# Six products without weight sums at the head of the first block, and weight parts of two pairs made one product later

## The chip, the cores and the metric

The kernel runs on one core of one Trainium2 chip. The metric is the device time of one execution in microseconds; several executions are made, and their median is given. Times inside an execution come from the hardware profiler and count from the start of the span.

## The reference

The program is a bidirectional encoder trunk of two layers on 512 tokens plus 16 learned meta tokens, with 1024 channels. Each layer is a feed-forward block, a mixer of two parallel branches (gated linear attention and grouped-query attention), and a second feed-forward block. The change touches the feed-forward block alone:

```python
def swiglu(x, w_gate, w_up, w_down):
    return (jax.nn.silu(x @ w_gate) * (x @ w_up)) @ w_down

h = h + 0.5 * swiglu(rmsnorm(h, norm_gains[l, 0]), ffn_w_gate[l, 0], ffn_w_up[l, 0], ffn_w_down[l, 0])
h = h + mixer(rmsnorm(h, norm_gains[l, 1]), ...)
h = h + 0.5 * swiglu(rmsnorm(h, norm_gains[l, 2]), ffn_w_gate[l, 1], ffn_w_up[l, 1], ffn_w_down[l, 1])
```

The hidden width is 2816, which is 22 tiles of 128 columns. The kernel works them as 11 pairs; a pair is two hidden tiles, gate and up.

## The kernel before

Each float32 matmul is made of three matmuls in a faster format: an operand is split into a high part (`whi` for a weight, made by ScalarE, L227) and a low part (`wlo`, made by VectorE from the weight and the high part, L228), and high by high, high by low and low by high are summed in PSUM.

For gate and up of a pair, the weight is cut into four blocks 11, 12, 21, 22, and the tokens into two halves. Instead of eight block products, seven are formed, by a Winograd scheme. They are called 1 to 7. Products 1, 2 and 4 use the blocks 11, 12 and 22 as they come from HBM (`DIRECT`). Products 5, 6, 7 and 3 use sums and differences of blocks. Those sums are built in SBUF: ScalarE writes the negative of block 11 or 12 (L178), SP loads a base block (L173), and the GpSimd queue issues DMAs that add a block or another sum onto it (L183). For one pair the chain is: negative of 11, add 21 to it (this is the weight of 7), add that to a loaded 22 (the weight of 6), add 22 to a loaded 21 (the weight of 5), and add the weight of 6 to the negative of 12 (the weight of 3). Each of these transfers is 512 KB.

One product is 24 matmuls of TensorE (L516) into two PSUM banks. Of a pair, products 1, 6, 7 and 4 add up in the same banks X; ScalarE copies X out after 1, 6 and 7 (`snapshot`, L522). Product 2 has banks Y. Products 5 and 3 add up in banks Z; before 3 may start, VectorE has read Z together with the copy that was made after 7 (L534). `hidden` then applies the norm factor `rs`, the gate function and the product, and splits the result for the down projection (L393). PSUM holds two double banks for even pairs (`s2`) and two for odd ones (`ss`).

The norm factor `rs` of the block is made from the squares of the input (ScalarE L427, added up by VectorE L431), a matmul with a constant (L399), and a few steps on ScalarE and VectorE (L405, L376, L409 to L411). The opening block computes the squares at product 5 of pair 0.

`ffn_steps` lists the products and the down projection's steps of a block; the same list makes the plan of weight loads, in the order of use. When product j is emitted, `Weights.use` emits the making of the parts of all products before j + `AHEAD_MADE` (4) and the loads of all before j + `AHEAD_FETCHED` (6). `whi` and `wlo` have four buffers each, raw weights three, the negatives three, the loaded bases two. A scheduler then orders each engine's queue; the engines work their queues in order.

In this text 1·6 is product 6 of pair 1, and so on. The first of a block's groups has the pairs 0 to 3.

Of the kernel before, what the change touches and what calls it, by code (L numbers as in the profile page):

```python
# [14 lines left out]
ALU = mybir.AluOpType  # L15
AX = mybir.AxisListType

P = 128
D = 1024
KC = D // P  # L20
# [13 lines left out]
AHEAD_MADE = 4  # L34
# [11 lines left out]
DIRECT = {"1": "11", "2": "12", "4": "22"}  # L46


def ffn_steps():


    steps, pair = [], 0
    for g, n in enumerate(GROUPS):

        ahead = g == 0
        steps += [("P", p, c) for p in range(pair, pair + 1 + ahead) for c in "12"]
        steps += [("P", pair, c) for c in "65"]
        for i in range(n):
            p, more = pair + i, i + 1 < n
            early = [[("P", p + 1, "1")], [("P", p + 1, "2")]] if more else \  # L60
                [[("D", g, 0, 0, 2 * n - 2)], [("D", g, 1, 0, 2 * n - 2)]]
            if ahead and i == 0:
                early = [[], []]
            steps += early[0] + [("P", p, "7")] + early[1] + [("P", p, "4"), ("P", p, "3")]
            if more:
                steps += [("P", p + 1, "6"), ("P", p + 1, "5")]
        steps += [("D", g, m, 0, 2 * n - 2) for m in range(2, HELD)]
        steps += [("D", g, m, 2 * n - 2, 2 * n) for m in range(HELD)]
        steps += [("D", g, m, 0, 2 * n) for m in range(HELD, KC)]
        pair += n  # L70
    return steps


def weight_plan():


    plan = []

    def mat(name, idx, col, k0, nk, width=P):
        for k in range(k0, k0 + nk):  # L80
            plan.append(("tile", name, idx, k * P, col, width))

    def ffn(l, f):
        for step in ffn_steps():
            if step[0] == "P":
                plan.append(("op", (l, f)) + step[1:])
            else:
                _, g, m, first, last = step
                mat("ffn_w_down", (l, f), m * P, 2 * sum(GROUPS[:g]) + first, last - first)

    gate_cols = [c + m * P for m in range(KC) for c in (O_GA, O_GB)]
    for l in range(DEPTH):
        ffn(l, 0)
        cols = [O_R + i * P for i in range(4)]
        for c in cols:
            mat("w_in", (l,), c, 0, KC)
# [12 lines left out]
    return plan  # L109
# [38 lines left out]
class Weights:  # L148
# [83 lines left out]
            if not isinstance(load, int) and load[2] in "12":  # L232
                self.sums(*load, w)

    def use(self, j):
        self.make(j + AHEAD_MADE)
        self.fetch(j + AHEAD_FETCHED)
        return self.got[j]

# [15 lines left out]
        self.pos += n - 1  # L255
        return [t[:, c : c + n * width] for t in self.got[self.at[s]]]

    def op(self, *load):

        assert PLAN[self.pos][1:] == load, (PLAN[self.pos], load)  # L260
        self.pos += 1
        return [t.rearrange("p (w k m) -> p w k m", w=2, k=KC // 2) for t in self.use(self.at[load])]


def build(tc, ctx, xt, wts, win, par, w2, const, umask, out):
    nc = tc.nc
    V, S, G, TE = nc.vector, nc.scalar, nc.gpsimd, nc.tensor
# [10 lines left out]
    W = Weights(nc, pool("wraw", 3), pool("whi", 4), pool("wlo", 4), wts, win)  # L278
# [217 lines left out]
    def ffn(l, f, norm, done, following):  # L496

        x, rs, n = norm.x, None, live[0]
        w = n // 2
# [3 lines left out]
        def product_of_pair(p, product):  # L503
            kind = "s2" if p % 2 == 0 else "ss"
            st = made.setdefault(p, {})
            where, begin = {"1": ("X", 1), "6": ("X", 0), "7": ("X", 0), "4": ("X", 0), "2": ("Y", 1), "5": ("Z", 1),
                            "3": ("Z", 0)}[product]
            if begin:
                st[where] = pair(kind == "s2")
            acc = st[where][:, :, :w]  # L510
            hi, lo = W.op((l, f), p, product)
            at = PLACE[product]
            for k, (xh, xl) in enumerate(x):
                for j in range(2):
                    for i, (a, b) in enumerate(((hi, xh), (hi, xl), (lo, xh))):
                        TE.matmul(acc[:, j], a[:, j, k], b[:, at], start=bool(begin and k == 0 and i == 0),  # L516
                                  stop=k == len(x) - 1 and i == 2, skip_group_check=not begin)

            def snapshot(name):
                t = slots["snap"].tile([P, T], F32, tag="snap", name=nm("snap"))[:, :n]  # L520
                st[name] = v2(t)
                S.copy(st[name], acc)  # L522

            if product == "1":
                snapshot("p1")
            elif product == "2":
                c = slots["c"].tile([P, 4 * T], F32, tag="c", name=nm("c"))[:, : 4 * n]
                st["c"] = c.rearrange("p (j q c) -> p j q c", j=2, q=4)
                V.tensor_tensor(st["c"][:, :, 0], st["p1"], acc, ALU.add)
            elif product == "6":  # L530
                snapshot("q")
            elif product == "7":
                snapshot("r")
                V.tensor_tensor(st["c"][:, :, 3], st["r"], st["Z"][:, :, :w], ALU.add)  # L534
            elif product == "4":
                hidden(st, p, 1)
            elif product == "3":
                V.tensor_tensor(st["c"][:, :, 1], st["q"], acc, ALU.add)
                hidden(st, p, 0)

        def hidden(st, p, m):

            c = st["c"]
            t, u = [c[:, j, 2 * m : 2 * m + 2].rearrange("p q c -> p (q c)") for j in range(2)]
            x21 = st["X"][:, :, :w]
            cuts = [(t, u, t, u, slice(0, n))] if m == 0 else \
# [28 lines left out]
            if g == len(GROUPS) - 1:  # L575
                (done or finish_chunk)(m)

        steps = ffn_steps()
        last_op = max(i for i, t in enumerate(steps) if t[0] == "P")
        for i, step in enumerate(steps):  # L580
            if step[0] == "P":
# [596 lines left out]
```

## Time and profile before

| what | us |
|---|---|
| median of three runs | 2242.1 (2241.26 to 2243.97) |
| the profiled execution's own time | 2245.28 |
| its span on the profiler | 2243.5 |
| TensorE busy / idle in the span | 2199.7 / 43.8 |
| VectorE, ScalarE, GpSimd busy | 1522.7, 1196.9, 154.1 |
| mean granted TensorE clock | 0.995 |

A row of the page or of a timeline names the engine, the line, the operation, what it writes and reads (`ss<-xc,whi` is a product of input parts and a weight's high part into PSUM), the shape and the count; in square brackets stands how long the engine was idle before it and what ended that. PEld is the weight load of TensorE, SPq and ACTq are DMA issues. A row of stretches gives the stretch, its length, and for PE, PEld, DVE, ACT and POOL the busy time and the number of instructions, then the granted clock, the busy share of the DMA engines and GB/s. `w<-win` is a weight block from HBM, `s<-w` and `w<-s` are transfers between sums. Line numbers are those of the kernel before; the changed kernel has the same lines some 3 to 13 further on.

### The profile page before, as it was taken

To read this page: it belongs to the slowest core of one execution; us is meant where nothing else is said; L and a number is where in the kernel's file an instruction comes from. 1 tells how busy PE (TensorE), PEld (TensorE's weight loads), DVE (VectorE), ACT (ScalarE), POOL (GpSimd) and SP (SyncE) were. 2 spreads that over 40 slices of the span, in tenths; PEclk is the share of its full clock that TensorE was granted. 3 is DMA by queue.
4 is the path that set the end of the run, shared out by engine and by line. 5 is a ranking of instruction groups with operands and counts; after the bars stand their busy time and mean duration, and the time that the engine had idled before them with its cause. 6 is when DMAs were issued, how large, how long until landed. Compare 5 with 4: busy or idle time off the path is not lost.

```text
span 2243.5 us, 39771 instructions
## 1 busy us (share of the span) xinstructions
PE 2199.7 (98%) x16506; PEld 2094.6 (93%) x16506; DVE 1522.7 (68%) x2415; ACT 1196.9 (53%) x1769; POOL 154.1 (7%) x180
## 2 busy tenths in 40 slices
PE   6999999999999999999999999999999999999998
PEld 5999999989999999999999999999788888989897
DVE  6656567586886676565696575675878767756566
ACT  7635355454785564454575363553457836636353
POOL 1101010000000010101011110100000001101010
PEclk9999999999999999999999999999999999999999
DMA  9859563212113475766667685632121136859662
GB/s 252 217 151 221 150 175 99 85 48 70 48 40 110 132 201 157 189 178 179 171 173 198 162 220 140 173 105 76 52 80 48 48 123 170 215 149 226 152 177 66
DMA packets 88613, 315.58 MB, mean 141 GB/s; under 512 B 9840, under 2 KB 12272, under 8 KB 88432
## 3 DMA queue, kind: packets, MB, share of 16 engines
q1 hardware_dynamic: 61136, 218.26, 29.2%
q0 software_dynamic: 25344, 92.29, 23.0%
q8 instruction: 129, 2.11, 0.4%
q10 hardware_dynamic: 1952, 2.50, 0.3%
q14 instruction: 52, 0.43, 0.1%
HBM read 264.77 MB, written 2.10 MB: 119 GB/s over the span
## 4 chain that ended last, share of the span: by engine, by line
PE 86%; DVE 6%; ACT 4%; DMA 2%; issue 1%; SPq 0%; DVEq 0%; ACTq 0%; POOLq 0%
PE ss L516 37%; PE ss L393 26%; PE mm L393 13%; PE sm L393 2%; DMA w<-win 2%; DVE wlo L228 1%; PE sm L893 1%; PE ss L868 1%; ACT whi L227 1%; ACT t L376 1%; PE sm L909 1%; PE sm L910 1%; PE ss L869 1%; PE ss L399 1%; PE sm L718 0%
## 5 line engine op out<-in xcount | busy, mean ns | idle before, releaser
L516 PE MATMUL ss<-xc,whi 128*128 128x264 f32 (+1 forms) x4928 | 905.4, 285 | 22.7 <-ACT whi L227 14.9
L516 PEld LDWEIGHTS ss<-xc,whi 128*128 128x128 f32 x4928 | 768.1, 189 | 27.2 <-ACT whi L227 15.3
L516 PE MATMUL ss<-xc,wlo 128*128 128x264 f32 (+1 forms) x2464 | 702.3, 285 | 3.8 <-DVE wlo L228 3.8
L393 PE MATMUL ss<-g,whi 128*128 128x264 f32 (+2 forms) x2692 | 495.3, 300 | 0.0
L516 PEld LDWEIGHTS ss<-xc,wlo 128*128 128x128 f32 x2464 | 466.5, 189 | 5.9 <-DVE wlo L228 5.6
L393 PEld LDWEIGHTS ss<-g,whi 128*128 128x128 f32 x2692 | 391.4, 188 | 16.2
L393 PE MATMUL mm<-x,whi 128*128 128x264 f32 (+1 forms) x1712 | 384.5, 315 | 0.0
L227 ACT CAST whi<-w 128x1024 fp32r<-128x1024 f32 (+1 forms) x221 | 231.0, 1046 | 265.4 <-PE ss L393 117.7
L227 ACT CAST whi<-raw 128x1024 fp32r<-128x1024 f32 x190 | 199.4, 1049 | 292.8 <-PE mm L393 97.5
L228 DVE TENSOR_TENSOR wlo<-w,whi 128x1024 fp32r<-128x1024 f32 (+1 forms) x221 | 267.9, 1219 | 110.3 <-ACT whi L227 108.5
L393 PE MATMUL ss<-g,wlo 128*128 128x264 f32 (+2 forms) x1346 | 312.2, 300 | 0.0
L228 DVE TENSOR_TENSOR wlo<-raw,whi 128x1024 fp32r<-128x1024 f32 x190 | 232.2, 1222 | 95.5 <-ACT whi L227 94.0
L393 PEld LDWEIGHTS mm<-x,whi 128*128 128x128 f32 x1712 | 278.3, 188 | 16.6 <-issue 1.0
L393 PE MATMUL mm<-x,wlo 128*128 128x264 f32 (+1 forms) x856 | 265.9, 315 | 0.0
L393 PEld LDWEIGHTS ss<-g,wlo 128*128 128x128 f32 x1346 | 215.7, 188 | 8.3
L227 ACT CAST whi<-s 128x1024 fp32r<-128x1024 f32 x88 | 92.5, 1051 | 151.1 <-PE ss L516 131.4
L228 DVE TENSOR_TENSOR wlo<-s,whi 128x1024 fp32r<-128x1024 f32 x88 | 107.6, 1223 | 96.2 <-ACT whi L227 96.1
L393 PEld LDWEIGHTS mm<-x,wlo 128*128 128x128 f32 x856 | 159.5, 188 | 8.4 <-issue 0.7
L483 DVE SCALAR_TENSOR_TENSOR t<-ss,rs 128x528 f32<-128x528 f32 (+1 forms) x93 | 64.6, 701 | 127.1 <-PE ss L393 127.0
L178 ACT ACTIVATE s<-w 128x1024 f32<-128x1024 f32 x88 | 93.3, 1060 | 74.7 <-DMA w<-win 40.4
L183 POOL DMA_DIRECT2D w<-win x44 | 39.1, 889 | 944.7 <-DVE wlo L228 439.5
L522 ACT COPY snap<-ss 128x528 f32<-128x528 f32 (+1 forms) x132 | 77.1, 584 | 1.2 <-PE ss L516 1.2
(245 smaller groups left out, 2568.7 us busy)
## 6 DMA issues: line engine op xcount, KB each, us to landing
w<-win SPq DMA_DIRECT2D x219, 512.0 KB, 4.7
raw<-wts SPq DMA_DIRECT2D x190, 512.0 KB, 3.4
s<-win POOLq DMA_DIRECT2D x44, 512.0 KB, 6.8
w<-s POOLq DMA_DIRECT2D x44, 512.0 KB, 5.5
w<-win POOLq DMA_DIRECT2D x44, 512.0 KB, 7.2
s<-w POOLq DMA_DIRECT2D x44, 512.0 KB, 7.4
h<-xt SPq DMA_DIRECT2D x3, 528.0 KB, 6.9
out<-h ACTq DMA_DIRECT2D x4, 256.0 KB, 2.3
```

Source lines behind the costliest of these rows:

```text
L178: self.nc.scalar.activation(t, w, AF.Copy, scale=-1.0)
L183: self.nc.gpsimd.dma_start(t, src, accum_op=ALU.add)
L227: nc.scalar.copy(hi[:, cs], w[:, cs])
L228: nc.vector.tensor_tensor(lo[:, cs], w[:, cs], hi[:, cs].bitcast(F32), ALU.subtract)
L376: prev_act[0] = S.activation(*args, **kw).ins
L393: TE.matmul(acc.half[i][:width], lhs, rhs[:, acc.spans[i]], start=first, stop=last)
L399: TE.matmul(a, weights, x[:, hs], start=True, stop=True)
L483: V.scalar_tensor_tensor(cut(dst[rows]), pv[rows], -0.5 * f, cut(rs[rows]), ALU.mult, ALU.mult)
L516: TE.matmul(acc[:, j], a[:, j, k], b[:, at], start=bool(begin and k == 0 and i == 0), stop=k == len(x) - 1 and i == 2, skip_group_check=no ...
L522: S.copy(st[name], acc)
L868: TE.matmul(s[:n, i, :HF], lhs, kh[:, hs], start=True, stop=False)
L869: TE.matmul(s[:n, i, :HF], lhs, kl[:, hs], start=False, stop=True)
```

## The change

`ffn_steps` gets a flag that is set for the first block of the program alone. There, product 4 of pairs 0 and 1 stands right behind products 1 and 2 of both pairs, so that the block begins with 0·1, 0·2, 1·1, 1·2, 0·4, 1·4. Such a product 4 can't be added onto X, which holds product 1 alone at that time. It is summed in banks of its own (W), ScalarE copies it out, and after product 7 VectorE adds the copy of X to it; `hidden` of that half follows product 7 and reads the sum from SBUF. Besides, in pairs 0 and 1 of every block the parts are made one product later (`AHEAD_MADE` - 1). The core of the diff:

```diff
-def ffn_steps():
+def ffn_steps(opening):
...
         steps += [("P", p, c) for p in range(pair, pair + 1 + ahead) for c in "12"]
+        early4 = (0, 1) if opening and ahead else ()
+        steps += [("P", p, "4") for p in early4]
         steps += [("P", pair, c) for c in "65"]
...
-            steps += early[0] + [("P", p, "7")] + early[1] + [("P", p, "4"), ("P", p, "3")]
+            steps += early[0] + [("P", p, "7")] + early[1] + [("P", p, c) for c in "43" if c == "3" or p not in early4]
...
-    def use(self, j):
-        self.make(j + AHEAD_MADE)
+    def use(self, j, ahead=AHEAD_MADE):
+        self.make(j + ahead)
         self.fetch(j + AHEAD_FETCHED)
...
+            apart = product == "4" and "r" not in st
...
+            if apart:
+                where, begin = "W", 1
...
-            hi, lo = W.op((l, f), p, product)
+            hi, lo = W.op((l, f), p, product, ahead=AHEAD_MADE - (p < 2))
...
+            elif apart:
+                S.copy(st["c"][:, :, 2], acc)
+                st["apart"] = True
             elif product == "7":
                 snapshot("r")
                 V.tensor_tensor(st["c"][:, :, 3], st["r"], st["Z"][:, :, :w], ALU.add)
+                if "apart" in st:
+                    V.tensor_tensor(st["c"][:, :, 2], st["c"][:, :, 2], st["r"], ALU.add)
+                    hidden(st, p, 1)
...
-            cuts = [(t, u, t, u, slice(0, n))] if m == 0 else \
+            cuts = [(t, u, t, u, slice(0, n))] if m == 0 or "apart" in st else \
...
-        steps = ffn_steps()
+        steps = ffn_steps((l, f) == (0, 0))
```

What stands in the engines' queues then, at the places that matter. TensorE before, behind 0·7 (whi6): whi9 is 1·6, L399 the norm's sums, whi7 is 0·4.

```order
L516 MATMUL ss25_242<-xc22_215,whi6_344 128x264
L516 MATMUL ss25_242<-xc21_214,wlo6_345 128x264
L516 MATMUL ss29_310<-xc3_104,whi9_467 128x264
L516 MATMUL ss29_310<-xc4_105,whi9_467 128x264
L399 MATMUL ss44_457<-t34_404,const_84 128x264 x2
L516 MATMUL ss25_242<-xc3_104,whi7_374 128x264
L516 MATMUL ss25_242<-xc4_105,whi7_374 128x264
```

Two matmuls of 1·6 and the norm's sums stood ahead of 0·4. TensorE with the change, where 1·6 (whi10) ends and 0·3 (whi9) begins:

```order
L523 MATMUL ss29_310<-xc21_214,whi10_527 128x264
L523 MATMUL ss29_310<-xc22_215,whi10_527 128x264
L523 MATMUL ss29_310<-xc21_214,wlo10_528 128x264
L523 MATMUL ss44_485<-xc3_104,whi9_486 128x264
L523 MATMUL ss44_485<-xc4_105,whi9_486 128x264
L523 MATMUL ss44_485<-xc3_104,wlo9_487 128x264
```

1·6 now stands whole behind 0·7 and ahead of 0·3, and the norm's sums have moved up into 0·5. ScalarE before: whi9 is 1·6, whi10 is 1·5, snap46 the copy of X after 0·7, s3 the negative that begins the sums of pair 2, rs and t the norm factor.

```order
L227 CAST whi8_428<-s4_00_0_171 128x1024
L227 CAST whi9_467<-w22_00_1_205 128x1024
L227 CAST whi10_500<-w21_00_1_247 128x1024
L522 COPY snap46_497<-ss25_242 128x528
L178 ACTIVATE s3_00_2_544<-w11_00_2_471 128x1024
L405 ACTIVATE rs43_456<-ss44_457,eps_88 128x528
```

ScalarE with the change: whi10 is 1·6, whi11 is 1·5, whi12 is 2·1, snap48 the copy of X after 0·7.

```order
L230 CAST whi10_527<-w22_00_1_205 128x1024
L408 ACTIVATE rs45_516<-ss46_517,eps_88 128x528
L181 ACTIVATE s3_00_2_611<-w11_00_2_490 128x1024
L379 ACTIVATE rs45_516<-rs45_516 128x528
L230 CAST whi11_569<-w21_00_1_278 128x1024
L412 ACTIVATE t47_523<-rs45_516 128x528
L230 CAST whi12_607<-w11_00_2_490 128x1024
L529 COPY snap48_555<-ss25_242 128x528
```

Between the cast of 1·6 and the copy after 0·7 stood one cast; now six instructions stand there. SP before, from the raw block of 0·4 on: the two blocks ending in _205 and _247 are the bases for the sums of pair 1, w11 and w12 of pair 2 the weights of 2·1 and 2·2, w22_00_1_588 the raw block of 1·4.

```order
L173 DMA w22_00_0_315<-win 128x1024
L173 DMA w11_00_2_471<-win 128x1024
L173 DMA w22_00_1_205<-win 128x1024
L173 DMA w21_00_1_247<-win 128x1024
L173 DMA w12_00_2_550<-win 128x1024
L173 DMA w22_00_1_588<-win 128x1024
```

SP with the change, from the raw block of 0·4 on; the second row is the raw block of 1·4, and the bases for the sums of pair 1 are now _205 and _278.

```order
L176 DMA w22_00_0_243<-win 128x1024
L176 DMA w22_00_1_245<-win 128x1024
L176 DMA w11_00_2_490<-win 128x1024
L176 DMA w12_00_2_573<-win 128x1024
L176 DMA w22_00_1_205<-win 128x1024
L176 DMA w21_00_1_278<-win 128x1024
L176 DMA w11_00_3_713<-win 128x1024
```

The raw block of 1·4 moved up to the second place, and the blocks of 2·1 and 2·2 both stand ahead of the bases of pair 1.

More of the change, by code (lines that the diff above doesn't have):

```diff
@@ L83, in ffn @@
     def ffn(l, f):
-        for step in ffn_steps():
+        for step in ffn_steps((l, f) == (0, 0)):
             if step[0] == "P":
@@ L256, in row, with op @@
         return [t[:, c : c + n * width] for t in self.got[self.at[s]]]
-    def op(self, *load):
+    def op(self, *load, ahead):
         assert PLAN[self.pos][1:] == load, (PLAN[self.pos], load)
         self.pos += 1
-        return [t.rearrange("p (w k m) -> p w k m", w=2, k=KC // 2) for t in self.use(self.at[load])]
+        return [t.rearrange("p (w k m) -> p w k m", w=2, k=KC // 2) for t in self.use(self.at[load], ahead)]
 def build(tc, ctx, xt, wts, win, par, w2, const, umask, out):
```

## The prediction

> **What bounds the kernel now.** I read the page first, then the list of waits of TensorE, then the opening in the timelines of each engine.
>
> ```profile
> span 2243.5 us, 39771 instructions
> PE 2199.7 (98%) x16506; PEld 2094.6 (93%) x16506; DVE 1522.7 (68%) x2415; ACT 1196.9 (53%) x1769; POOL 154.1 (7%) x180
> ```
>
> TensorE bounds the kernel: it idles 43.8 of 2243.5 us. The change takes no matmul away, so it can only work on that idle time and on matmuls that run at half clock behind it. The longest wait of TensorE in the first 80 us (us in total, times, longest):
>
> ```profile
> PE ss L516 <- ACT whi L227: 14.9, 3, 7.4
> ```
>
> One of its three parts is the first 7.4 us of the program, before any weight is there. Another is one hole in the middle of pair 0. TensorE's timeline there (start, length, instruction), with the first matmul of the down projection (L393) as a mark for later:
>
> ```profile
> 37.79 0.28 PE L516 MATMUL ss<-xc,wlo 128*128 128x264 f32 x1
> 45.07 0.81 PE L516 MATMUL ss<-xc,whi 128*128 128x264 f32 x2 [7.00 <-ACT whi L227]
> 45.68 1.96 PE L399 MATMUL ss<-t,const 128*128 128x264 f32 x4
> ...
> 48.97 0.42 PE L516 MATMUL ss<-xc,wlo 128*128 128x264 f32 x1
> ...
> 49.63 0.42 PE L516 MATMUL ss<-xc,wlo 128*128 128x264 f32 x1
> ...
> 52.95 0.40 PE L516 MATMUL ss<-xc,whi 128*128 128x264 f32 x2
> ...
> 53.31 0.41 PE L516 MATMUL ss<-xc,whi 128*128 128x264 f32 x2
> ...
> 102.81 0.65 PE L393 MATMUL ss<-g,whi 128*128 128x264 f32 x4
> ```
>
> Three matmuls take 0.66 us from 48.97 to 49.63, so 0.22 us each, and 0.36 us from 52.95 to 53.31, so 0.122 us each. The same stretches as sums, with the granted clock behind POOL's column:
>
> ```profile
> 38.10:45.00 6.90, 0.00 (x0) 0.00 (x0) 2.41 (x3) 1.29 (x2) 0.72 (x2) 0.81 0.87 178
> 42.50:52.60 10.10, 6.80 (x25) 5.85 (x26) 4.39 (x5) 5.42 (x7) 1.76 (x2) 0.50 0.63 142
> 52.70:57.00 4.30, 4.30 (x37) 4.30 (x37) 2.48 (x4) 1.74 (x2) 0.00 (x0) 1.00 0.87 210
> ```
>
> The idle 7 us brought 10 us at half clock with them. The price of the hole: from 37.9 to 102.81 TensorE does 18 products of 24 matmuls, 432 × 0.122 = 52.7 us, and the norm's sums (L399: 1.96 us at half clock, so about 1.0 at full). That is 53.7 us of work in 64.9 us: 11.2 us are lost. ScalarE's timeline says what was waited for:
>
> ```profile
> 43.97 1.04 ACT L227 CAST whi<-w 128x1024 fp32r<-128x1024 f32 x1 [5.61 <-DMA w<-s]
> 46.77 1.04 ACT L227 CAST whi<-w 128x1024 fp32r<-128x1024 f32 x1 [1.75 <-DMA w<-win]
> 47.72 0.59 ACT L522 COPY snap<-ss 128x528 f32<-128x528 f32 x1
> 48.21 1.06 ACT L178 ACTIVATE s<-w 128x1024 f32<-128x1024 f32 x1
> 49.17 0.69 ACT L405 ACTIVATE rs<-ss,eps 128x528 f32<-128x528 f32 x1
> 49.89 0.64 ACT L376 ACTIVATE rs<-rs 128x528 f32<-128x528 f32 x1
> 50.57 0.64 ACT L409 ACTIVATE t<-rs 128x528 f32<-128x528 f32 x1
> ```
>
> The cast at 43.97 makes the high part of product 6 of pair 1 (written 1·6 from here). Its weights are a sum that a DMA of the GpSimd queue adds up (w<-s), and that landed only then. TensorE stands in front of it because the order puts two matmuls of 1·6 ahead of 0·4 and 0·3, as the rows shown with the change have it.
>
> **The change, part by part.** The opening: 0·4 and 1·4 use no sum. They now stand fifth and sixth, each in banks of its own, so TensorE has two more products before it needs 1·6. Until 26 us nothing differs. Their raw weights take the next two places of SP's queue: the first is the same transfer as before, the second takes the place of a later weight:
>
> ```profile
> 21.45 0.33 SPq L173 DMA_DIRECT2D w<-win  x1
> w<-win SPq DMA_DIRECT2D x16, 512.0 KB, 7.2
> ```
>
> With the opening's median of 7.2 us it lands at 28.7. ScalarE then makes the high parts of 1·4, 0·6 and 0·5 back to back, 0.95 us from start to start (46.77 to 47.72 above), and VectorE the low parts, 1.14 us apart (32.55 to 33.69):
>
> ```profile
> 32.55 1.22 DVE L228 TENSOR_TENSOR wlo<-w,whi 128x1024 fp32r<-128x1024 f32 x1
> 33.69 0.70 DVE L431 TENSOR_TENSOR t<-t,t 128x528 f32<-128x528 f32 x1
> 34.79 3.96 DVE L431 TENSOR_TENSOR t<-t,t 128x528 f32<-128x528 f32 x5 [0.40 <-ACT t L427]
> 51.24 0.71 DVE L410 SCALAR_TENSOR_TENSOR t<-ss,t 128x528 f32<-128x528 f32 x1 [1.06 <-ACT t L409]
> 51.99 0.71 DVE L411 SCALAR_TENSOR_TENSOR rs<-t,rs 128x528 f32<-128x528 f32 x1
> ```
>
> 1·4's low part is there at 28.7 + 1.04 + 1.22 = 31.0, ahead of its turn at 31.9; 0·5's, with two low parts and one addition more, at about 33.8, ahead of 37.9. So TensorE passes 37.9 without a stop, seven products done as before. From there it goes step by step.
>
> 0·5 and the norm's sums: the sums stand behind 8 of 0·5's 24 matmuls (38.9) and wait for seven additions of squares. VectorE starts these at 33.7, with one low part (1.14) among them: 33.7 + 7 × 0.79 (3.96/5) + 1.14 = 40.3. TensorE waits 1.4 us; 0 to 2 if the squares come sooner or later. Then follow 1.0 for the sums, 16 × 0.122, and 24 × 0.122 for 0·7: TensorE reaches 1·6 at 46.2.
>
> 1·6: its sum's base now stands behind two loads in SP's queue that used to come after it. The GpSimd queue and its transfers before:
>
> ```profile
> 36.26 0.86 POOL L183 DMA_DIRECT2D w<-s  x1 [9.21 <-DMA w<-win]
> 33.50:38.00 4.50, 4.50 (x38) 4.36 (x36) 3.73 (x6) 4.50 (x9) 1.35 (x2) 1.00 1.01 373
> w<-s POOLq DMA_DIRECT2D x1, 512.0 KB, 7.6
> s<-w POOLq DMA_DIRECT2D x1, 512.0 KB, 4.6
> ```
>
> The adding DMA left at 36.26, when the base had landed. Two loads of 512 KB at 373 GB/s are 2.8 us, less some 0.2 because the queue starts sooner: it leaves at 38.9. It took 7.6 us beside hardware loads; an add with little beside it took 4.6. Now one load is left, almost done by then, so I take 4.6: the sum lands at 43.5 (46.5 with 7.6). The high part is ready at 44.6: no wait, and 1·6 ends at 49.15.
>
> 0·3 is what comes late next. It adds onto the banks of 0·5, and VectorE must first read these together with ScalarE's copy of 0·7. On ScalarE six instructions now stand between the cast of 1·6 and that copy, where one cast stood. From the sum's landing L, with the distances of the ScalarE rows above: 0.95 + 0.72 + 0.96 + 0.68 = L + 3.3 for the cast of 1·5, which ends at L + 4.35. VectorE goes on in order: its low part 1.14, two steps of the norm factor 0.75 + 0.71, the low part of 2·1 1.14, the addition that frees the banks 0.70, so L + 8.9. With L = 43.5 that is 52.4, and TensorE is free from 49.15: it waits 3.25 us (6.2 with L = 46.5; under 1 only with L under 41).
>
> The clock: a like wait stands at the start of the last block, and a shorter one in the second:
>
> ```profile
> 1908.21 0.50 PE L516 MATMUL ss<-xc,whi 128*128 128x256 f32 x2 [2.48 <-ACT snap L522]
> 1909.60:1912.90 3.30, 3.30 (x18) 3.30 (x17) 0.61 (x2) 0.43 (x1) 0.00 (x0) 0.50 0.87 302
> 810.70:812.00 1.30, 0.00 (x0) 0.00 (x0) 0.46 (x1) 1.30 (x2) 0.00 (x0) 1.00 0.97 132
> 812.10:816.00 3.90, 3.90 (x32) 3.90 (x33) 2.15 (x4) 0.85 (x1) 0.00 (x0) 1.00 1.01 257
> ```
>
> 2.48 us idle brought 3.3 us at half clock; 1.3 us brought none. I count one such stretch: 3.3 × (1 − 0.122/0.22) = 1.5 us (0 to 4.5, which is 10.1 × 0.445, the hole's). The Trainium skill (TensorE: Matmul & The Clock Gate, "What's actually happening") lets the clock halve after at least one idle window of about 3.4 us; by that rule this wait would cost nothing more, and the time would be that of the first rival. The trace speaks against it: 2.48 us were enough at 1908.
>
> The rest of the edit: two copies on ScalarE (0.59 each, as L522) and two additions on VectorE (0.70 each, as L431) come in, two cut pieces go out. The copy of 0·4 frees the banks that 0·5 takes at about 34.2, 3.7 us early; without that cover 0·5 would wait for it. The sums of pair 2 start with ScalarE's negative at L + 1.7 and need two adds:
>
> ```profile
> s<-win POOLq DMA_DIRECT2D x3, 512.0 KB, 9.5
> w<-s POOLq DMA_DIRECT2D x3, 512.0 KB, 5.6
> ```
>
> With the hand-overs that is 62; TensorE wants 2·6 at about 72. It is hidden, and late only if the adds take 10 us more.
>
> Parts a product later holds for pairs 0 and 1 of all four blocks. In the second and the last block every engine's order is the same row for row, so the waits at 810 and 1908 stay: 0. In the third, one part moves behind the squares, and the norm's sums stand 8 matmuls earlier, about 1.0 us. They waited there already:
>
> ```profile
> PE ss L399 <- DVE t L431: 0.5, 1, 0.5
> ```
>
> The additions they wait for end sooner by that one low part, 1.14, too: 0, at most 0.6 either way.
>
> **The sum.** Lost before 11.2; after 1.4 + 3.25 + 1.5 = 6.2. Gain 5.0 us: the mark of 102.81 should come at 97.8. The profiled execution took 2245.28 us (span 2243.5), which becomes 2240.3; it lies 3.2 above the median of the runs, 2242.1, from which the gain gives 2237.1 us. A measurement of this kernel tells about 0.2%, 4.5 us, from no change: at or under 2237.6 is faster.
>
> **The rivals.** No half clock behind the new wait, because it is split or falls short: 1.5 us better, 2235.6. For it: 1.3 us idle cost none. Against it: the 2.48 us at 1908 did.
>
> The sum lands late, at 46.5, because its add takes 7.6 us as before. 1·6 starts at 47.6 and 0·3 at 55.4: losses 1.4 + 6.2 + 1.5 to 3, about 9.9; gain 1.3, 2240.8. For it: the 4.6 us were measured with no hardware load running. Against it: only one load is left beside this add.
>
> Slower than before: the two loads that moved ahead run beside pair 1's first add and slow each other:
>
> ```profile
> 28.00:31.00 3.00, 3.00 (x27) 3.00 (x26) 2.08 (x3) 2.73 (x4) 0.00 (x0) 1.00 1.07 203
> ```
>
> In these 3 us the adds alone filled the DMA engines at 203 GB/s. If the loads get half of that, each takes 5 us, the base leaves some 3 us later still (42.1), and with an add of 7.6 L is about 50. Then 0·3 starts at 58.9, a wait of 9.75; with 1.4 and 4.5 for the clock 15.7 are lost, 4.5 more than before: 2246.6. It decides from L of about 47. Against it: from 33.5 to 38 the loads got 373 GB/s as soon as that add was done. The Trainium skill (DMA: Bandwidth & Descriptors, "Queues, rings and completion order") has each DMA engine change between its queues packet by packet, which is this rival's mechanism; the 7.6 us beside 4.6 agree with it.
>
> That it does not do what it says is out: the order shows the six products at the head.
>
> **How the numbers follow.** My case 0.47, no half clock 0.17, the late sum 0.28, slower 0.06, something else 0.02. My case has ±1.5 us of its own, so three in five of it lie beyond 0.2%; with no half clock and a little of the rest that is 0.50 for faster. The remainder of my case and nearly all of the late sum lie within 0.2%: 0.44. Slower is 0.06. The range goes from 2233 (L = 42, no wait for the squares, no half clock) to 2241.5 (the late sum and most of one more us).
>
> **What would show it.** Right: TensorE without a stop from 26 to 38.9; the cast of 1·6 between 43 and 45; a wait of about 3 us near 50 for VectorE's addition (c, L544); a clock of 0.50 for one stretch only; the first L393 at 97 to 98. Wrong: 1·6 waiting for its cast, a first L393 after 101, or a changed wait in the second or last block.

## The result and the profile after

The changed kernel takes 2240.65 us in the median (2237.75 to 2245.16, 12 runs), the kernel before in the same comparison 2241.75 us (2240.48 to 2245.07, 12 runs). The ratio is 0.9993 with a 95% interval of 0.9986 to 1.0001: no change that the measurement can tell, as against 0.9978 in the forecast. A second comparison gave 0.9991 (0.9982 to 1.0000). The ratios in this text are estimated from the runs of a comparison; they need not be the quotient of its two medians.

The profiled execution of the changed kernel took 2245.16 us, that of before 2245.28. TensorE is busy 3.7 us longer and idles 40.0 us in place of 43.8:

```profile
span 2243.4 us, 39767 instructions
PE 2203.4 (98%) x16506; PEld 2098.2 (94%) x16506; DVE 1522.6 (68%) x2413; ACT 1197.0 (53%) x1771; POOL 154.0 (7%) x180
```

So the idle time went down as it should, but TensorE worked longer on the same 16506 matmuls, that is at a lower clock. In the opening the 7 us hole is gone. Here are three of TensorE's waits of the first 110 us (engine, tile, line, what was waited for, us, times, longest; the others lie ahead of 26 us or stay under 0.3) and its timeline, down to the first matmul of the down projection, which is L396 now and called the mark below:

```profile
PE ss L523 <- DVE c L544: 3.2, 1, 3.2
PE ss L523 <- DVE wlo L231: 1.8, 4, 0.6
PE ss L402 <- DVE t L434: 1.3, 1, 1.3
```

```profile
40.76 1.16 PE L402 MATMUL ss<-t,const 128*128 128x264 f32 x4 [1.26 <-DVE t L434]
47.55 0.39 PE L523 MATMUL ss<-xc,wlo 128*128 128x264 f32 x1 [0.50 <-DVE wlo L231]
53.67 0.59 PE L523 MATMUL ss<-xc,whi 128*128 128x264 f32 x1 [3.18 <-DVE c L544]
...
100.27 0.65 PE L396 MATMUL ss<-g,whi 128*128 128x264 f32 x4
```

The mark came from 102.81 to 100.27, a gain of 2.5 us where 5.0 had been worked out. Two of the three waits were forecast: the squares (1.26, forecast 1.4) and 0·3, which stands for VectorE's addition (3.18, forecast 3.25). The third, of 0.50 for the low part of 1·6, was not. What led to the wait of 0·3 is shown next: the adding transfer as GpSimd issued it, then what ScalarE and VectorE did before they came to that addition:

```profile
38.79 0.86 POOL L186 DMA_DIRECT2D w<-s  x1 [11.75 <-DVE t L434]
```

```profile
45.19 1.05 ACT L230 CAST whi<-w 128x1024 fp32r<-128x1024 f32 x1 [4.59 <-DMA w<-s]
46.14 0.70 ACT L408 ACTIVATE rs<-ss,eps 128x528 f32<-128x528 f32 x1
46.73 1.04 ACT L181 ACTIVATE s<-w 128x1024 f32<-128x1024 f32 x1
47.68 0.63 ACT L379 ACTIVATE rs<-rs 128x528 f32<-128x528 f32 x1
48.21 1.03 ACT L230 CAST whi<-w 128x1024 fp32r<-128x1024 f32 x1
49.15 0.64 ACT L412 ACTIVATE t<-rs 128x528 f32<-128x528 f32 x1
49.70 1.03 ACT L230 CAST whi<-w 128x1024 fp32r<-128x1024 f32 x1
50.63 0.59 ACT L529 COPY snap<-ss 128x528 f32<-128x528 f32 x1
```

```profile
52.92 0.70 DVE L544 TENSOR_TENSOR c<-snap,ss 128x528 f32<-128x528 f32 x1
```

The add left at 38.79 (forecast 38.9) and its sum was there at 45.2 (forecast 43.5); the transfer took 6.4 us instead of 4.6. From there the chain ran as worked out: copy of 0·7 at 50.63, addition done 8.4 us behind the sum (forecast 8.9). The clock column says the rest (stretch, length, busy time of PE, PEld, DVE, ACT, POOL, granted clock, DMA share, GB/s):

```profile
52.50:55.80 3.30, 2.13 (x9) 2.13 (x10) 3.27 (x5) 2.09 (x3) 0.00 (x0) 0.50 0.95 309
55.90:59.20 3.30, 3.30 (x17) 3.30 (x17) 0.21 (x1) 0.00 (x0) 1.73 (x2) 0.50 1.01 398
59.40:63.00 3.60, 3.60 (x32) 3.60 (x31) 3.29 (x6) 2.29 (x4) 0.00 (x0) 1.00 1.11 233
574.80:578.00 3.20, 3.20 (x16) 3.12 (x16) 2.42 (x9) 1.68 (x5) 0.00 (x0) 0.50 0.00 0
1905.90:1909.20 3.30, 2.23 (x10) 2.23 (x11) 2.25 (x3) 1.02 (x2) 0.00 (x0) 0.50 0.86 161
1909.40:1912.70 3.30, 3.30 (x18) 3.30 (x17) 0.20 (x1) 0.42 (x1) 0.00 (x0) 0.50 0.72 277
```

Two stretches at half clock stand behind the wait at 50 instead of one. Another lies at 575, where TensorE did not idle at all, and in the last block there are two where the kernel before had one. With 0.445 of such a stretch lost, the second one in the last block and the one at 575 cost 2 × 3.41 × 0.445 = 3.0 us more than before, which is as much as the mark had gained and somewhat over: this execution ends level with that of before.

### The profile page after: what moved, and what is told of

Read it like the earlier page. It is cut to its first block, busy times and chain, and to the rows that moved or that the text cites. A ratio compares the mean times of both kernels' runs of the same rounds, so it can differ in the third digit from the quotient of the medians.

```text
span 2243.4 us, 39767 instructions
## 1 busy us (share of the span) xinstructions
PE 2203.4 (98%) x16506; PEld 2098.2 (94%) x16506; DVE 1522.6 (68%) x2413; ACT 1197.0 (53%) x1771; POOL 154.0 (7%) x180
## 4 chain that ended last, share of the span: by engine, by line
PE 86%; DVE 6%; ACT 3%; DMA 3%; issue 1%; SPq 0%; DVEq 0%; ACTq 0%; POOLq 0%
PE ss L523 37%; PE ss L396 26%; PE mm L396 13%; PE sm L396 2%; DMA w<-win 2%; DVE wlo L231 1%; PE sm L906 1%; PE ss L881 1%; PE sm L922 1%; ACT t L379 1%; DMA w<-s 1%; PE sm L923 1%; ACT whi L230 1%; PE ss L882 1%; PE ss L402 0%
## 5 line engine op out<-in xcount | busy, mean ns | idle before, releaser
L396 PE MATMUL ss<-g,whi 128*128 128x264 f32 (+2 forms) x2692 | 495.3, 300 | 0.0
L396 PEld LDWEIGHTS ss<-g,whi 128*128 128x128 f32 x2692 | 391.4, 188 | 16.2
L396 PE MATMUL mm<-x,whi 128*128 128x264 f32 (+1 forms) x1712 | 385.4, 315 | 0.0
L230 ACT CAST whi<-raw 128x1024 fp32r<-128x1024 f32 x190 | 199.3, 1049 | 289.5 <-PE mm L396 97.8
L396 PE MATMUL ss<-g,wlo 128*128 128x264 f32 (+2 forms) x1346 | 312.1, 300 | 0.0
L396 PEld LDWEIGHTS mm<-x,whi 128*128 128x128 f32 x1712 | 279.1, 189 | 16.6 <-issue 1.0
L396 PE MATMUL mm<-x,wlo 128*128 128x264 f32 (+1 forms) x856 | 266.6, 316 | 0.0
L396 PEld LDWEIGHTS ss<-g,wlo 128*128 128x128 f32 x1346 | 215.7, 188 | 8.3
L396 PEld LDWEIGHTS mm<-x,wlo 128*128 128x128 f32 x856 | 160.0, 189 | 8.5 <-issue 0.7
```

The lines of the kernel that those rows point to most:

```text
L230: nc.scalar.copy(hi[:, cs], w[:, cs])
L396: TE.matmul(acc.half[i][:width], lhs, rhs[:, acc.spans[i]], start=first, stop=last)
```

## The experiments

Four of the experiments were run on another chip than the other eight: the two without adding transfers, the third buffer, and the copy first in every block. Each is compared with the kernel before on its own chip, whose median was 2243.84 us there, 2243.20 and 2243.23 us in the two comparisons on the first chip.

**What the sums cost at all.** Two kernels leave out the adding transfers of the first block, one from the changed kernel, one from the kernel before.

```diff
     def add(self, f, t, src):
+        if f == (0, 0):
+            return
         self.nc.gpsimd.dma_start(t, src, accum_op=ALU.add)
```

> The changed kernel with the adding transfers of the first block left out (the weights of products 7, 6, 5 and 3 there are then not the sums; all matmuls, casts and plain loads stay). Theory A (from 38 us to the first down projection only the sums hold TensorE up, and what is left is the wait for the squares): 37.9 + 53.7 us of work + 1.3 = a first down projection at 92.5 to 93.5, no wait of over 0.7 us between 42 and 93, no half clock there, and 6 to 8 us less than the changed kernel: ratio to the kernel before 0.9960 to 0.9970. Theory B (ScalarE's and VectorE's own work holds it up too): waits of 2 us or more stay near 50 us, the first down projection comes at 96 or later, ratio over 0.9975.

> The kernel before with the adding transfers of the first block left out in the same way. Theory A (the two kernels differ only in how they bear the lateness of the sums): first down projection at 92.5 to 94, as in the changed kernel without the adds, within 1 us of it in the median. Theory B (the change pays or costs something beside the sums: copies, two additions, the parts a product later): the two differ by 1.5 us or more at the first down projection.

Measured: ratio 0.9953 (0.9940 to 0.9967) for the changed kernel without the adds, 0.9957 (0.9943 to 0.9971) for the kernel before without them. The mark, and TensorE's busy time up to it, first of the changed kernel and then of before:

```profile
91.04 0.65 PE L398 MATMUL ss<-g,whi 128*128 128x264 f32 x4
37.90:91.00 53.10, 53.00 (x429) 52.59 (x429) 42.21 (x52) 35.85 (x46) 0.00 (x0) 1.00 0.42 137
```

```profile
91.26 0.65 PE L395 MATMUL ss<-g,whi 128*128 128x264 f32 x4
37.90:91.00 53.10, 53.10 (x432) 52.97 (x433) 41.32 (x53) 35.13 (x45) 0.00 (x0) 1.00 0.46 146
```

Theory A of both held in its mechanism, with marks over 1 us below its ranges: in the changed kernel even the wait for the squares is gone. Without sums both orders give the same mark within 0.2 us, at full clock and without a stop in the stretch shown. So all the time at stake here, 11.6 us before and 9.2 after, comes with the adding transfers; the copies, the two additions and the parts a product later cost TensorE nothing up to the mark. Leaving the transfers out does two things at once: no sum is late, and the plain loads have the DMA engines to themselves (from 16 to 95 us their median falls from 5.3 us in the changed kernel to 3.3). How much belongs to the second was not tried. About 10 of the 11.6 us arrive in the whole time (0.43 to 0.47% of 2243.8).

**Does one profile stand for the kernel?** Both kernels were run again as they are.

> The changed kernel once more. Theory (its opening is set by when the sums land, and that differs from execution to execution): the sum of pair 1 lands anywhere from 43.8 to 45.8 (as in the four profiled executions with this opening), the wait near 50 us is 2.5 to 3.5 us, the first down projection at 98 to 101, ratio to the kernel before 0.9985 to 1.0000. If the prediction's sum was right and the first profile was an unlucky one: a sum at 43.5, one stretch at half clock, the first down projection at 97.8, ratio 0.9978.

> The kernel before once more, one look. Theory (the hole near 38 us moves with the landing of the sum, which differs from execution to execution): the add lands at 41.5 to 46 instead of 43.9, the first down projection anywhere from 100.5 to 105. Rival (the opening repeats itself): 43.9 and 102.8 within 0.5 us.

Measured: the changed kernel 0.9991 (0.9982 to 1.0000), one run of the kernel before at 2241.01 us. TensorE's rows and a stretch of the changed kernel, then TensorE's rows of the kernel before:

```profile
53.49 0.62 PE L523 MATMUL ss<-xc,whi 128*128 128x264 f32 x2 [3.19 <-DVE c L544]
...
99.03 0.65 PE L396 MATMUL ss<-g,whi 128*128 128x264 f32 x4
...
53.80:57.10 3.30, 3.30 (x17) 3.30 (x16) 2.10 (x3) 0.64 (x1) 0.86 (x1) 0.50 0.97 366
```

```profile
43.91 0.81 PE L516 MATMUL ss<-xc,whi 128*128 128x264 f32 x2 [6.13 <-ACT whi L227]
...
101.29 0.65 PE L393 MATMUL ss<-g,whi 128*128 128x264 f32 x4
```

The theory of differing executions held. In the second execution of the changed kernel one stretch at half clock followed, not two, and the mark lies 1.2 us earlier. The hole of the kernel before was 6.1 us this time, not 7.0, and its mark 1.5 us earlier; in a third execution with the same queues up to there (the kernel before with another edit, below) it was 5.4 us and the mark 100.70:

```profile
42.81 0.81 PE L519 MATMUL ss<-xc,whi 128*128 128x264 f32 x2 [5.35 <-ACT whi L228]
...
100.70 0.65 PE L395 MATMUL ss<-g,whi 128*128 128x264 f32 x4
```

Three marks before, 102.81, 101.29 and 100.70, have a mean of 101.6; two after, 100.27 and 99.03, have one of 99.7. The gain of the opening is nearer 1.9 us than 5. That agrees with the two ratios (0.7 and 0.9 in a thousand, 1.6 and 2.0 us), though neither can be told from no change.

**The two halves of the change apart.** First the opening with the parts as early as before, then the parts alone.

```diff
-            hi, lo = W.op((l, f), p, product, ahead=AHEAD_MADE - (p < 2))
+            hi, lo = W.op((l, f), p, product, ahead=AHEAD_MADE)
```

```diff
-        for step in ffn_steps((l, f) == (0, 0)):
+        for step in ffn_steps(False):
...
-        steps = ffn_steps((l, f) == (0, 0))
+        steps = ffn_steps(False)
```

> The new opening with the parts of all pairs made as early as before. Theory (the opening is what moves the time, the parts a product later are worth nothing by themselves): TensorE still waits 3 to 3.5 us near 50 us for VectorE's addition before product 3 of pair 0, the first down projection comes at 100.3 +- 1, and the median is that of the changed kernel, 2240.65, within 1.5 us. Rival (the later parts carry the gain, because they free VectorE for the squares and ScalarE for the sums): the wait for the norm's sums grows from 1.3 to 2.4 us or the wait near 50 us to over 4, the first down projection comes at 102 or later, and the median is at 2242 or above.

> The parts of pairs 0 and 1 made a product later, the opening in its old order. Theory (worth nothing): the 7 us hole near 38 to 45 us stays, the first down projection comes at 102.8 +- 0.6, the median within 1 us of the kernel before, 2241.75. Rival (the later parts carry the gain): the first down projection at 101.5 or earlier and the median at 2240.5 or below.

Measured: 0.9993 (0.9985 to 1.0002) and 0.9993 (0.9984 to 1.0001). The opening alone:

```profile
54.38 0.81 PE L523 MATMUL ss<-xc,whi 128*128 128x264 f32 x2 [3.33 <-DVE c L544]
...
99.80 0.65 PE L396 MATMUL ss<-g,whi 128*128 128x264 f32 x4
```

The first theory held: the same wait and the same mark as the whole change. The parts alone have the hole in another shape (1.43, 1.53 and 1.25 us near 40), and then this:

```profile
69.08 0.81 PE L523 MATMUL ss<-xc,whi 128*128 128x264 f32 x2 [3.94 <-ACT snap L529]
...
103.56 0.65 PE L396 MATMUL ss<-g,whi 128*128 128x264 f32 x4
```

So both theories missed part of it: the rival's earlier mark did not come, and the mark lies 0.2 us above the first theory's range, but the hole did not stay; it was split and half of it came 25 us later. The medians of the two halves can't be told from each other or from no change.

**The queue on ScalarE.** The copy of 0·7 is put ahead of the cast of 1·5, by an order edge on ScalarE from that copy to the casts that are written at product 0·3.

```diff
+                with self.tc.issue_after(self.behind) if self.behind else nullcontext():
                     nc.scalar.copy(hi[:, cs], w[:, cs])
...
+            W.behind = st["r_ins"] if "apart" in st and p == 0 and product == "3" else None
```

> The changed kernel, with ScalarE's copy of product 7 of pair 0 queued ahead of the cast of product 5 of pair 1 in the opening; no transfer is moved. Theory A (product 3 of pair 0 waits for ScalarE's queue behind the late sum, not for the sum): the sum lands at 45.2 as in the changed kernel, yet the wait of 3.2 us for VectorE's addition is gone and with it both stretches at half clock (6.83 us, some 3.0 us lost): the first down projection at 94.1 (93.5 to 95.5), the median 6 us below the changed kernel, 2234.5 (2233 to 2237). Theory B (the late sums bound the stretch whatever the queue): TensorE waits about as long a little later, for the parts of products 6 or 5 of pair 1, the first down projection comes at 98 to 100 and the median at 2238.5 to 2241.

Measured: 0.9992 (0.9983 to 1.0001). The order also put 11 of the 24 matmuls of 1·6 behind 0·3. Here are TensorE's rows (products are L526, the down projection L398, the copy L532, the addition L547), and ScalarE's rows behind the third wait:

```profile
50.22 0.51 PE L526 MATMUL ss<-xc,whi 128*128 128x264 f32 x2 [1.93 <-DVE c L547]
...
67.47 0.51 PE L526 MATMUL ss<-xc,whi 128*128 128x264 f32 x2 [1.00 <-DVE c L547]
...
88.29 0.51 PE L526 MATMUL ss<-xc,whi 128*128 128x264 f32 x2 [3.00 <-ACT snap L532]
...
101.62 0.65 PE L398 MATMUL ss<-g,whi 128*128 128x264 f32 x4
```

```profile
86.69 1.04 ACT L231 CAST whi<-w 128x1024 fp32r<-128x1024 f32 x1 [5.81 <-DMA w<-s]
87.64 0.59 ACT L532 COPY snap<-ss 128x528 f32<-128x528 f32 x1
```

Theory B is nearer, though not by the products that it named. Product 0·3 started 3.5 us earlier than in the changed kernel and without half clock behind it, but TensorE then met the sum of pair 3, which landed at 86.6, with a copy queued behind its cast. The wait had moved 38 us down the block.

**The loads ahead of the bases.** The two loads of pair 2 are put behind the bases of pair 1 on SyncE, as they stood before the change.

```diff
+HOLD = (((0, 0), 2, "11"), ((0, 0), 2, "12"))
...
+            with self.tc.issue_after(self.last) if self.last and (f, i, name) in HOLD else nullcontext():
+                d = self.nc.sync.dma_start(w[:, a[0] : a[-1] + 1], self.dram(f, i, name)[:, a[0] : a[-1] + 1])
+            if (f, i, name, tag) == ((0, 0), 1, "21", "wsb"):
+                self.last = d.ins
```

> The changed kernel, with the two loads of pair 2 queued on SyncE behind the bases of pair 1's sums, as they were before the change. Theory A (the adding transfer is stretched by the second adding transfer that follows it 1.2 us behind, not by the loads): it leaves at 36.2 and takes 6.4 us again, the sum lands at 42.6, the wait for VectorE's addition shrinks from 3.2 to about 1.2 us, with no or one stretch at half clock: first down projection at 95.5 to 97.5, median 2236 to 2238. Theory B (loads beside it stretch it): it takes 7.6 us as in the kernel before and lands at 43.9, the wait is 2 to 2.5 us with one or two stretches at half clock, first down projection at 98 to 99.5, median 2238.5 to 2240.

Measured: 0.9999 (0.9989 to 1.0009). The issue of the add and the cast of its sum:

```profile
36.54 0.86 POOL L192 DMA_DIRECT2D w<-s  x1 [10.11 <-DVE wlo L237]
```

```profile
46.25 1.04 ACT L236 CAST whi<-w 128x1024 fp32r<-128x1024 f32 x1 [6.17 <-DMA w<-s]
```

The add left 2.2 us earlier and its sum landed 1.1 us later: 9.7 us, with both loads beside it. They landed at 41.1 and 43.0, as the order on SyncE has them, and the next load at 46.8. The second adding transfer left 3.0 us behind the first instead of 1.2, so theory A's cause is not it. Theory B's direction held and its size was too small. In this one execution, that is the mechanism of the prediction's slower rival (loads beside the add stretch it), here without a slower time: TensorE waited 3.7 us for the addition, the mark came at 101.51, the median did not move.

**A third buffer for the bases.** The room comes from ScalarE's copies and the norm factor.

```diff
-dict(g=16, t=6, rs=2)
+dict(g=16, t=6, rs=1)
...
-        pools = open_pools("left", psum=("s2",), c=2, snap=3, s2=2)
+        pools = open_pools("left", psum=("s2",), c=2, snap=2, s2=2)
...
-        pools = open_pools("left", wsa=3, wsb=2)
+        pools = open_pools("left", wsa=3, wsb=3)
```

> The changed kernel with a third buffer for the bases of the sums (to have the room, two buffers instead of three for ScalarE's copies and one instead of two for the norm factor). Theory A (the sums follow each other in a chain, each base waiting for the sum before it to have been read by an add, and so the sums of pair 3 land at 85 to 91 us whatever is done at product 3 of pair 0): the base of pair 1 loads before 30 us, its add leaves at about 34.5 and lands at 39 to 41, the wait of 3.2 us near 50 falls under 1, the sums of pair 3 land 3 us earlier or more, the first down projection at 94 to 96.5, the median 4 to 6 us below the changed kernel. Theory B (the adds themselves are the limit, 5 to 10 us each on one queue): the first sum lands earlier, but those of pair 3 within 1.5 us of 86.8 and 91.3, the first down projection at 98.5 to 101, the median within 1.5 us of the changed kernel.

Measured: 1.0020 (1.0009 to 1.0031), slower.

```profile
37.11 0.86 POOL L186 DMA_DIRECT2D w<-s  x1 [8.75 <-DMA s<-win]
```

Theory A fell. With its base early, the add waited for the first add of pair 1 instead, which had landed just before 37.11, and the sum was there at 44.2. For this add the limit is the pair's own adds, as theory B had it. Theory B's numbers did not come true either: the sum for product 6 of pair 3 landed at 90.6, 3.8 us later than in the changed kernel, and the mark came at 107.35, later than both theories said. How much of that is due to the fewer buffers of the copies was not tried.

**The copy first in every block.** The condition `"apart" in st` is left out of the order edge.

```diff
-            W.behind = st["r_ins"] if "apart" in st and p == 0 and product == "3" else None
+            W.behind = st["r_ins"] if p == 0 and product == "3" else None
```

> The changed kernel with ScalarE's copy of product 7 of pair 0 ahead of the cast of product 5 of pair 1 in all four blocks. Theory A (in the last block the copy only stands behind a cast whose sum is late): the wait of 2.7 us at 1904 falls under 0.7 and the half clock behind it goes (3.41 or 6.83 us, 1.5 to 3.0 us lost), the one of 1.3 us at 808 too; median 4 to 6 us below that of the run with the copy first in the opening alone, ratio to the kernel before 0.9965 to 0.9975. Theory B (the late sums then stop TensorE a little later in the same block, as they did at 85 us in the opening): a wait of 1.5 us or more comes up within 40 us behind, the end of the block moves by under 1.5 us, ratio 0.9985 to 0.9995.

Measured: 0.9965 (0.9951 to 0.9978), 2233.94 us in the median of five runs (2233.05 to 2237.72) beside 2243.84 of the kernel before. First the wait in the last block as the changed kernel has it; then ScalarE with this edit, which copies before the cast whose sum is late:

```profile
1906.97 0.79 PE L523 MATMUL ss<-xc,whi 128*128 128x256 f32 x2 [2.70 <-ACT snap L529]
```

```profile
1896.29 0.59 ACT L532 COPY snap<-ss 128x512 f32<-128x512 f32 x1 [0.92 <-PE ss L526]
1898.81 1.05 ACT L231 CAST whi<-w 128x1024 fp32r<-128x1024 f32 x1 [1.94 <-DMA w<-win]
```

TensorE's wait for the copy there (2.70 us in the changed kernel, 2.24 with the copy first in the opening only) is gone, none of over 0.5 us comes up within 40 us behind, and no half clock stands there. Theory A held. The queues of the opening are the same, row for row, as in the run with the copy first there alone, and yet its sum of pair 3 landed at 83.0 rather than 86.6, TensorE met no wait at 85, and the mark came at

```profile
96.76 0.65 PE L398 MATMUL ss<-g,whi 128*128 128x264 f32 x4
```

4.9 us before that of the same queues in another execution, on the other chip. On one chip the marks of the kernel before lie 0.6 us apart, over all three executions 2.1. So a single profile can be off by as much as the gain looked for; whether the chip has a part in the 4.9 us was not tried.

**The copy first, without the change.** The same edge in the kernel before.

> The kernel before (neither the new opening nor the parts a product later), with ScalarE's copy of product 7 of pair 0 ahead of the cast of product 5 of pair 1 in all blocks. Theory A (the wait in the last block is worth 4 to 6 us in either kernel, and the change's opening some 2 to 3 us more on top): ratio to the kernel before 0.9975 to 0.9985, that is 2 us or more above the changed kernel with the copy first. Theory B (the change is worth nothing, the copy all): ratio 0.9960 to 0.9970, as the changed kernel with the copy first (0.9965).

Measured: 1.0002 (0.9994 to 1.0011), and the last block still has its wait:

```profile
1906.12 0.51 PE L519 MATMUL ss<-xc,whi 128*128 128x256 f32 x2 [2.52 <-ACT snap L525]
```

This run can't tell the theories apart, since the edge had no hold: with the parts made as early as before, the cast of 1·5 is written at 0·4, ahead of the place where the edge begins, and ScalarE's queue came out as it was. The parts a product later are what lets the edge work. What the copy first would bring to the kernel before stays open.

**The norm factor first too.** On top of the copy first in all blocks, the cast of 1·6 is queued behind the norm factor's steps, which need no sum.

```diff
+            squared[0] = S.activation(u, y, AF.Square).ins
...
+            W.behind = st["r_ins"] if p == 0 and product == "3" else \
+                squared[0] if (l, f, p, product) == (0, 0, 0, "7") else None
```

> The changed kernel with the copy of product 7 ahead in all blocks, and in the opening the norm factor's steps on ScalarE ahead of the cast of product 6 of pair 1, in the idle time in which ScalarE waits for the sum. Theory A (product 3 of pair 0 waits only for the queue on ScalarE and VectorE): its wait of 1.7 to 1.9 us near 48 us falls under 0.5, with no half clock behind it, the first down projection at 93.5 to 95.5 where the later sums are in time, the median 2 to 3 us below the version without it: ratio 0.9952 to 0.9958. Theory B (the sums of pairs 2 and 3 take it back): waits of over 1 us near 66 or 85 us, median within 1 us of that version, ratio 0.9962 to 0.9968.

Measured: 0.9976 (0.9967 to 0.9985), 2238.39 us. The wait of 0·3 is gone altogether (none of over 0.5 us between 42 and 64), and the block has it later (products are L527):

```profile
65.69 0.52 PE L527 MATMUL ss<-xc,whi 128*128 128x264 f32 x2 [0.95 <-DVE c L548]
...
87.73 0.81 PE L527 MATMUL ss<-xc,whi 128*128 128x264 f32 x2 [4.19 <-ACT snap L533]
...
102.22 0.65 PE L398 MATMUL ss<-g,whi 128*128 128x264 f32 x4
```

Theory B held for the opening. The sum of pair 3 landed at 86.1 and a mark of 102.2 came out of the best start of all. The median lies above that of the copy first alone, but the two intervals meet.

This run has the same edge in the later blocks as the one before the last, on the other chip, and that tells the edge from the chance in the opening. From the mark to the end of the span the two executions took 2133.5 and 2134.4 us; the twelve profiled executions without the edge there, or where it had no hold, took 2137.3 to 2143.1, 2140.1 in the mean. So the copy first is worth some 6 us behind the mark on either chip, where the waits of the second and the last block are gone in both. What sets the two apart lies ahead of the mark.

## Why the prediction was right or wrong

**The result** lies in the range, within 0.2%, at the edge that the late sum gave. The likeliest case was not what happened: it promised 5.0 us, and some 2 arrived. The interval includes no change at all.

**The mechanism** was right. TensorE passes from 26 to 39 us without a stop of over half a microsecond, the hole is filled, and 0·3 is late next, behind six instructions on ScalarE. The chain from the sum to the freed banks took 8.4 us (worked out: 8.9, though its terms add up to 8.8), the wait 3.18 (3.25), the wait for the squares 1.26 (1.4). That the wait of 0·3 came out so close is partly luck: the banks were free 1.2 us later than worked out, and 1·6 ended 1.3 us late as well (50.5 instead of 49.15), because the squares and its low part were late. The second and the last block kept their waits (1.30 us near 809, 2.70 at 1904) as said.

**The step that failed first: what was lost before.** The 11.2 us are those of one execution, and I took them off the median. The profiled execution lay 3.2 us above that median, and its hole was the longest of the three that are known now (7.0, 6.1, 5.4 us). Against the marks without adds, the kernel before loses 11.6, 10.0 and 9.4 us, 10.3 in the mean.

**The second: the adding transfer.** I took 4.6 us from the one row of another kind of add. In this opening it took 6.4 us, in the five other executions that have the new opening and leave its loads and buffers alone 4.5 to 6.8 (from GpSimd's issue to the landing). The page of before has a better row, the group over the whole program:

```profile
w<-s POOLq DMA_DIRECT2D x44, 512.0 KB, 5.5
```

With 5.5 the sum would have come at 44.4, and the sum of losses out 0.9 us higher. The sum landed 1.7 us late, half-way to the late rival, and that rival's time (2240.8) is the nearest to the result. That is luck too: its transfer of 7.6 us and its wait of 6.2 us did not happen, and part of the shortfall lay in the first step. Product 0·3 started at 53.67 and 53.49 in place of 52.4. Of the 3.1 us that are missing at the mark, 1.2 lie in the first step (101.6 against 102.81) and 1.9 in this one and the next (99.7 against 97.8).

**The third: the half clock.** One stretch was forecast, with 0 to 4.5 us as ends; one execution had two, the other one, 2.5 and 1.5 us. Whether there are one or two is set by how the wait falls on the clock's stretches, which the last section shows. The Trainium skill (TensorE: Matmul & The Clock Gate, "What's actually happening") has a free-running window of 3.41 us, and the trace agrees: each stretch at half clock in these runs is 3.41, 6.83 or 10.24 us long, up to the end stage. Its rule of a whole idle window is not what the runs show: the wait of the first execution lay over two windows, 1.96 us idle in the one and 1.22 in the other, and the clock was halved twice.

**What the sum did not have: the end of the chain.** I stopped at 0·3 and took the rest of the block as free. It is not. The sum for product 6 of pair 3 landed between 82.0 and 86.8 us in eleven of the twelve profiled executions with adds, and at 90.6 with the third buffer, however early TensorE came. Why it keeps this time is argued and not shown: each pair's adds stand in line behind those of the pair before. The row for it stands in ScalarE's timeline of before, at the cast of that sum:

```profile
88.25 1.05 ACT L227 CAST whi<-w 128x1024 fp32r<-128x1024 f32 x1 [1.40 <-PE ss L516]
```

It waited for TensorE to free a buffer, and the trace has its sum landing at 84.65: 3.6 us of slack, so that what is gained at 0·3 beyond that runs into the sum. That is where the copy first in the opening and the norm factor first lost theirs; in the run with the copy first in all blocks the sum came at 83.0 and nothing was lost there.

**The slower rival** (loads beside the add) has its mechanism in the run with the bases first: 9.7 us instead of 6.4. It agrees in direction with the rule of the Trainium skill that each DMA engine changes between its queues packet by packet (DMA: Bandwidth & Descriptors, "Queues, rings and completion order"); no run here shows how the packets of the two queues took turns. In the changed kernel it did not happen, because the two loads had landed at 35.6 and 36.9, before the add left at 38.79.

## What to carry to other kernels

Before a hole's whole length is booked as a gain, follow the supply that made it to its last link: here a chain of adding transfers delivered the last weights of pair 3 at 82 to 87 us whatever stood at the head of the block, and in two of three runs a wait taken away near 50 us came back at 65 and 88. Where queues are in order, put the short instruction that frees a buffer ahead of the one that waits for a transfer; on top of the change, that one edge was worth more (from 0.9993 to 0.9965) than the new order of products. And take a term's size from several executions or from a group over the program, since one profile put the same queues' mark at 96.8 and another, on another chip, at 101.6.

## What the runs showed of the hardware

The stretches at half clock lie on a grid of 3.41 us that runs on through the program; worked out on that grid from TensorE's records of the 14 executions, after the first 15 us and ahead of the last 40, a stretch with 1.9 us or more of idle time was followed by one at half clock each time, one with 0.9 to 1.56 us never, and between them it went both ways (1.60 us brought it, 1.84 did not). While the clock is halved, 0.6 us of idle time was enough for another such stretch, and one with at most 0.25 us ended it. So a wait of 3.2 us cost one stretch or two, by how it fell. Twice (at 575 us, in the changed kernel and with the bases first) a stretch came at half clock with no idle time ahead of it; why is not known.

An adding transfer of 512 KB within SBUF took 4.4 to 9.7 us at one and the same place of the program, longest in the run with the bases first, in which four plain loads ran beside it.
